# Layer 0's up-projection by Strassen's seven products, activations through DRAM, down-projection as a stage of its own

## The chip, the cores and the metric

One core of a Trainium2 chip runs the whole program as one launch. The metric is device time in microseconds (us): the median of the runs, beside a profile of one execution. Engines: PE is TensorE's matmul, PEld its weight load, DVE is VectorE, ACT is ScalarE, POOL is GpSimd, SP issues most of the DMAs.

## The reference, cut to what matters

Two layers work on 512 latent tokens and 256 context tokens with a model width of 1024. Each layer has a token mixing part (gated linear attention, window attention, pooling, one output projection) and a channel mixing part. Only the second is touched:

```python
def conv_ffn(h, w_up, conv_w, conv_b, w_down):      # h: tokens x 1024, w_up: 1024 x 5632, w_down: 2816 x 1024
    u = h @ w_up
    up = jnp.pad(u, ((0, 0), (1, 1), (0, 0)))
    u = up[:, :-2] * conv_w[0] + up[:, 1:-1] * conv_w[1] + up[:, 2:] * conv_w[2] + conv_b
    a, g = jnp.split(u, 2, axis=-1)
    return (jax.nn.silu(g) * a) @ w_down
...
h2 = rms_norm(x, norm2_g) * (1 + sc2) + sh2
x = x + g2 * conv_ffn(h2, w_up, conv_w, conv_b, w_down)
```

In layer 0 this runs over latents and context; in layer 1 over latents alone, since the context is no longer wanted. All data are float32.

## The kernel before, in words

Activations lie feature-major: a tile has 128 features on the partitions and the tokens along the free dimension, 512 latent columns and then 258 for the context (256 with a zero on either side, which the convolution needs). A float32 product is done in three passes of TensorE's rounded float32 type: each operand is split into a rounded part (hi) and the rest (lo), and hi*hi, hi*lo and lo*hi are added up in PSUM (acc3, L540). A weight tile is 128 x 1024: SP loads it into wst, ACT copies it to whi with rounding, DVE subtracts to wlo (wjob, L497). The normed activations are split when they are made (make_h, L763).

The channel mixing of layer 0 goes by 22 pairs j of a value tile and a gate tile (128 columns of w_up each). A pair takes two steps, one for each half of the 1024 rows (up, L1845; pairjob, L531). A step has 2 tiles x 4 k-tiles x 3 passes, and each of those is one matmul on the 512 latent columns and one on the 258 context columns: 96 matmuls a pair. Then conv (L1813) takes the tile out of PSUM (one ACT instruction for the middle tap and the bias, two on DVE for the outer taps), up_done (L1830) applies SiLU on ACT, multiplies on POOL, and splits the product into ahi (ACT) and alo (DVE), which stay in SBUF. After each group of pairs (FF_GROUPS: 2, 4, 4, 4, 4, 4) down_chunk (L1850) multiplies the group by its rows of w_down and adds the result to the residual x in SBUF; the pairs run two ahead of the groups (N_UP). Products go to three pairs of PSUM banks in turn (nbb3, L253). Between these steps stand single chunks of the modulation product of layer 1 (tick, L634: one 512 KB load and 32 x 128 columns on TensorE), which accumulate in a seventh bank. Before the first pair, norm2 (L1791) works out 1/rms and make_h the eight pairs of tiles of h; after the last group next_stats (L1911) sums the squares for the next norm.

Two things set the order. From the start to norm2, and from next_stats on, the tensor engine keeps the order of emission, which the kernel plans with estimated times; within the channel mixing (ordered(False) to ordered(True), L1928) the framework's scheduler orders every engine at compile time by its own estimate. Steps load their weights two jobs ahead (run_steps, L471, AHEAD). All SBUF tiles of 770 columns are slabs of one pool of 44 (slab, L218); a slab is free when its last reader is done. Weight rings and tables are constant tiles.

Of the kernel before, what the change touches and what calls it, by code (L numbers as in the profile page):

```python
# [8 lines left out]
F32 = mybir.dt.float32  # L9
# [5 lines left out]
ALU = mybir.AluOpType  # L15
# [16 lines left out]
SW = 770  # L32
# [33 lines left out]
N_WHI = 3  # L66
AHEAD = 2
# [5 lines left out]
FF_GROUPS = (2, 4, 4, 4, 4, 4)  # L73
LAT = slice(0, 512)
# [14 lines left out]
class Estimate:  # L89
    """Estimated times (us) of the engines and of the columns of the tiles. They only serve to choose  # L90
    an order of emission on the tensor engine in which it seldom waits."""
# [30 lines left out]
    def last(self, ap, kinds, eng=None):  # L122
        """time at which the last access (kinds: w, r) to the columns of ap is over, as seen by eng"""
# [21 lines left out]
class Engine:  # L145
    """An engine whose instructions also advance its estimated clock."""
# [27 lines left out]
    def _account(self, fname, args, kw):  # L174
# [22 lines left out]
        # what waits for a load lets the others pass  # L197
# [8 lines left out]
def trunk_kernel(ctx: ExitStack, tc: tile.TileContext, a, out, dbg=None):  # L206
# [6 lines left out]
    slabs = ctx.enter_context(tc.tile_pool(name="slabs", bufs=NSLAB))  # L213
    tiny = ctx.enter_context(tc.tile_pool(name="tiny", bufs=3))
# [6 lines left out]
    class Ring:  # L221
        """Fixed buffers taken in turn; reuse is ordered by the accesses themselves."""
# [9 lines left out]
    wad = Ring(const, N_WAD, 1024, F32, "wad")  # L232
    whi = Ring(const, N_WHI, 1024, F32R, "whi")
    wlo = Ring(const, N_WHI, 1024, F32R, "wlo")
    wst = Ring(const, N_WST, 1024, F32, "wst")
# [8 lines left out]
    class Pair:  # L244
        """latent and context halves of a product; whole where they lie in one tile"""
# [15 lines left out]
    # ---------------------------------------------------------------- constants  # L261
# [8 lines left out]
    scanm = const.tile([128, 512], F32, name="scanm")  # L270
    rope_c = const.tile([128, 4, 64], F32, name="rope_c")
    rope_s = const.tile([128, 4, 64], F32, name="rope_s")
    inve = const.tile([128, 2, 33], F32, name="inve")
    zbuf = const.tile([128, 512], F32, name="zbuf")
    G.memset(zbuf, 0.0)
# [3 lines left out]
    def load_tables():  # L279
        def load(**kw):  # L280
            after(SP.dma_start(**kw), start["il"])
        load(out=rope_c, in_=a["k_cos"].rearrange("(t p) d -> p t d", p=128))
        load(out=rope_s, in_=a["k_sin"].rearrange("(t p) d -> p t d", p=128))
# [6 lines left out]
        load(out=scanm, in_=a["k_scan"])  # L290
# [11 lines left out]
    gqk = const.tile([128, 512], F32, name="gqk")  # L302
    sink = const.tile([128, 6], F32, name="sink")
    nsink = const.tile([128, 6], F32, name="nsink")
    xdram = dram.tile([KD, 128, XW], F32, name="xdram")

    # ---------------------------------------------------------------- helpers
    def rstd_act(ss, inv_n, n=None):
        """(ss * inv_n + eps)^-0.5 from ScalarE's logarithm and exponential, refined by one step"""
# [46 lines left out]
    def warm(t):  # L356
        """keeps the tensor engine's clock up until t: idle, it falls to half its rate"""
# [545 lines left out]
    def layer(l):  # L903
# [946 lines left out]
        def down_chunk(j0, nk, mp, final):  # L1850
            def fn(hi, lo):
                if final:
                    bnext.load(3)
# [178 lines left out]
```

## Time and profile before

| | |
|---|---|
| median of 3 runs | 1647.62 us (1647.1 to 1647.99) |
| span of the profiled execution | 1645.8 us |
| TensorE busy / granted clock | 1607.5 us (98%) / 0.995 |
| VectorE, ScalarE, GpSimd busy | 947.4, 639.1, 268.4 us |
| channel mixing of layer 0 on TensorE | 401.7 to 971.9 us |

The profiled execution's own time is its span, from its first to its last instruction; the times of the runs hold a little more, 1647.62 - 1645.8 = 1.8 us at the median. A busy TensorE in this profile is not one at its peak, since the ends of matmuls are modelled: the pace is read from the distance of their starts. Start, duration and count stand in the rows of a timeline; a row "x2" merges two instructions.

### The profile page before, as it was taken

The page shows a single profiled execution, that of the slowest core. Times are in us where ns is not written, and L with a number is a line of the kernel's source. Part 1 is how long each engine was busy: PE and PEld are TensorE (multiplying, and loading weights), DVE is VectorE, ACT ScalarE, POOL GpSimd, SP SyncE. Part 2 cuts the span into 40 slices and gives each one's busy share as a digit, 9 for nine tenths or more (in the row PEclk, how much of TensorE's full clock was granted, in tenths as well). Part 3 has the DMA queues.
Part 4 walks back from the last instruction along what each step waited for, and adds up shares of the span by engine and source line. Part 5 has one row for each costly group of instructions (what it writes and reads, how often), then busy time and mean ns, then how long its engine had stood idle before and what let it go on. Part 6 is the DMA issues. An engine that isn't in the chain of part 4 may idle for free. (4 is left out here: it accounts for less than half of the span.)

```text
span 1645.8 us, 24715 instructions
## 1 busy us (share of the span) xinstructions
PE 1607.5 (98%) x9659; PEld 1308.3 (79%) x9659; DVE 947.4 (58%) x1730; ACT 639.1 (39%) x1174; POOL 268.4 (16%) x342
## 2 busy tenths in 40 slices
PE   7999999999999999999999999999899999999998
PEld 4777778787878888888888876778777888888886
DVE  6576477876554434434344364877785655545555
ACT  4354254554322313223132342654564433433331
POOL 1105034434100101001010041121302000000000
PEclk9999999999999999999999999999999999999999
DMA  9943352214243122221222275223232233233322
GB/s 324 236 146 112 114 161 59 81 40 154 77 130 89 64 65 65 65 65 52 64 64 65 89 252 156 62 67 112 66 104 78 70 110 103 91 95 97 102 90 77
DMA packets 206977, 169.12 MB, mean 103 GB/s; under 512 B 30616, under 2 KB 183715, under 8 KB 206860
## 3 DMA queue, kind: packets, MB, share of 16 engines
q1 hardware_dynamic: 204364, 158.74, 32.4%
q0 software_dynamic: 2496, 8.79, 1.5%
q8 instruction: 76, 1.25, 0.3%
q14 instruction: 41, 0.34, 0.1%
HBM read 160.15 MB, written 7.35 MB: 102 GB/s over the span
## 5 line engine op out<-in xcount | busy, mean ns | idle before, releaser
L155 ACT CAST whi<-wst 128x1024 fp32r<-128x1024 f32 (+3 forms) x202 | 201.2, 997 | 416.6 <-PE dbl L367 253.3
L155 DVE TENSOR_TENSOR wlo<-wst,whi 128x1024 fp32r<-128x1024 f32 (+1 forms) x177 | 218.0, 1232 | 181.9 <-ACT whi L155 179.8
L367 PE MATMUL dbl<-hlo,whi 128*128 128x512 f32 (+1 forms) x720 | 219.7, 357 | 0.0
L367 PE MATMUL dbl<-hhi,wlo 128*128 128x512 f32 x720 | 219.2, 357 | 0.0
L367 PE MATMUL dbl<-hhi,whi 128*128 128x512 f32 x720 | 218.2, 358 | 0.0
L155 POOL TENSOR_TENSOR cv<-cv 128x770 f32<-128x770 f32 (+1 forms) x44 | 69.4, 1578 | 816.1 <-ACT cv L155 806.2
L367 PE MATMUL sgl<-hhi,whi 128*128 128x512 f32 (+1 forms) x568 | 192.0, 367 | 1.0 <-ACT hhi L155 1.0
L367 PE MATMUL sgl<-hlo,whi 128*128 128x512 f32 (+1 forms) x568 | 186.3, 355 | 0.0
L367 PE MATMUL sgl<-hhi,wlo 128*128 128x512 f32 (+1 forms) x568 | 185.3, 355 | 0.0
L155 DVE SCALAR_TENSOR_TENSOR cv<-dbl,cwT,cv 128x769 f32<-128x769 f32 (+1 forms) x120 | 105.9, 883 | 58.7 <-ACT cv L155 56.7
L367 PEld LDWEIGHTS dbl<-hhi,whi 128*128 128x128 f32 x720 | 120.3, 189 | 22.8 <-issue 1.6
L367 PEld LDWEIGHTS dbl<-hlo,whi 128*128 128x128 f32 x720 | 120.1, 188 | 21.3
L367 PEld LDWEIGHTS dbl<-hhi,wlo 128*128 128x128 f32 x720 | 119.6, 188 | 21.0 <-issue 0.4
L367 PEld LDWEIGHTS sgl<-hhi,whi 128*128 128x128 f32 x568 | 100.1, 188 | 27.5 <-issue 10.4
L155 DVE SCALAR_TENSOR_TENSOR x<-dbl,modT,x 128x256 f32<-128x256 f32 (+1 forms) x105 | 65.2, 648 | 89.7 <-PE dbl L367 89.2
L367 PEld LDWEIGHTS sgl<-hlo,whi 128*128 128x128 f32 x568 | 100.5, 189 | 15.9 <-issue 0.5
L367 PEld LDWEIGHTS sgl<-hhi,wlo 128*128 128x128 f32 x568 | 100.2, 189 | 15.8
L367 PE MATMUL dbl<-alo,whi 128*128 128x512 f32 x342 | 103.8, 358 | 0.0
L367 PE MATMUL dbl<-ahi,whi 128*128 128x512 f32 x342 | 103.7, 358 | 0.0
L367 PE MATMUL dbl<-ahi,wlo 128*128 128x512 f32 x342 | 103.7, 358 | 0.0
L155 DVE TENSOR_TENSOR alo<-cv,ahi 128x770 fp32r<-128x770 f32 (+1 forms) x44 | 36.3, 825 | 110.2 <-ACT ahi L155 110.2
L155 DVE SCALAR_TENSOR_TENSOR x<-sgl,modT,x 128x256 f32<-128x256 f32 (+1 forms) x88 | 55.0, 641 | 54.0 <-PE sgl L367 53.5
(276 smaller groups left out, 2890.2 us busy)
## 6 DMA issues: line engine op xcount, KB each, us to landing
wst<-in_w_up SPq DMA_DIRECT2D x176, 256.0 KB, 3.3
adaw<-in_w_ada SPq DMA_DIRECT2D x96, 256.0 KB, 5.3
wad<-in_w_ada SPq DMA_DIRECT2D x48, 512.0 KB, 3.8
wst<-in_w_down SPq DMA_DIRECT2D x40, 512.0 KB, 3.4
wst<-in_w_in SPq DMA_DIRECT2D x26, 512.0 KB, 4.0
wst<-in_w_out SPq DMA_DIRECT2D x32, 192.0 KB, 3.3
xdram<-x SPq DMA_DIRECT2D x8, 385.0 KB, 6.0
x<-xdram POOLq DMA_DIRECT2D x8, 385.0 KB, 4.6
```

Of the source, the lines that this page charges most:

```text
L155: r = real(*args, **kw)
L367: T.matmul(o, w, m, start=start, stop=stop, **kw)
```

## The change

- The product for pairs 3 to 21 is a 2 x 2 block product: the rows of w_up in two halves, the value and the gate tile as the two columns, and the tokens in two halves of 386 columns (latents 0 to 385; latents 386 to 511, a zero, the context, a zero). Strassen's scheme (Winograd's form) takes seven products of blocks for the eight of the plain one, each of 4 k-tiles x 3 passes on 386 columns, and pays with sums: four of weights (S1 to S4) on GpSimd, four of activations (T1 to T4, made once), and per pair seven of results on the way out of PSUM. Pairs 0 to 2 run as plain products on the same 386 columns, while T1 to T4 are made.
- S1 to S4 are split into hi and lo like the weights X11, X12 and X22: 3584 columns a pair are cast and subtracted, where it was 2048.
- The activation of a pair is no longer split at once: it goes to DRAM (adram, by GpSimd's queue). The residual x goes to DRAM as well (xdram) while the norm is applied. After the last pair, all is loaded again by SP's queue; the activations are split then, and the down-projection runs in three groups (8, 8, 6).
- Weight rings and four tables share a pool of 13 tiles of 128 x 1024. In the Strassen stage its tiles hold the weights and their sums; the tables are loaded again afterwards. Weights are loaded one job ahead in that stage. The modulation chunks run in the plain steps and in the down-projection.
- Layer 1 keeps its code.

```diff
+        def make_y(R):
...
+            for k in range(KD):
+                SP.dma_start(out=xdram[k], in_=xs[k][:, 0:XW])
+            for p in range(4):
+                r, q = p // 2, p % 2
+                t1, t2 = f[r, q] = new7(f"Y{r + 1}1"), new7(f"Y{r + 1}2")
+                for i in range(2):
+                    k, o = 2 * p + i, HH * i
+                    for g, t, c, x in ((0, t1, o, slice(0, HH)), (0, t2, o, slice(HH, 512)), (1, t2, o + 513 - HH, CTX)):
+                        d = t[:, c:c + x.stop - x.start]
+                        V.scalar_tensor_tensor(d, in0=xs[k][:, x], scalar=amod[l][:, g, 1, k:k + 1], in1=R[:, x],
+                                               op0=ALU.mult, op1=ALU.mult)
+                        A.activation(d, d, func=AF.Identity, bias=modT[l][:, g, 24 + k:25 + k])
...
+        def products7(bank, w, n):
+            for k in range(4):
+                (wh, wl), (yh, yl) = w[k], yk(n, k)
+                for i, (w_, m_) in enumerate(((wh, yh), (wh, yl), (wl, yh))):
+                    mm(bank, w_, m_, start=k == 0 and i == 0, stop=k == 3 and i == 2)
...
+        def job7(j):
+            def load():
...
+                for half in range(2):
+                    t = wide(name="raw")
+                    for m, c0 in enumerate((128 * j, FF + 128 * j)):
+                        SP.dma_start(out=t.rearrange("p (k m n) -> p k m n", k=4, m=2)[:, :, m, :],
+                                     in_=rows(w_up, 512 * half, 4, c0, 128))
...
+                def split(src, h, l_):
+                    A.copy(h, src)
+                    V.tensor_tensor(l_, src, h.bitcast(F32), op=ALU.subtract)
...
+                split(xa[:, :, 0, :], cut(ua[:, 0:512]), cut(la[:, 0:512]))
+                G.tensor_tensor(q1, xa[:, :, 1, :], xb[:, :, 1, :], op=ALU.add)
+                G.tensor_tensor(q2, q1, xa[:, :, 0, :], op=ALU.subtract)
+                G.tensor_tensor(q4, xb[:, :, 0, :], q2, op=ALU.subtract)
+                G.tensor_tensor(q3, xa[:, :, 0, :], xa[:, :, 1, :], op=ALU.subtract)
...
+                split(s14[:, :], h14[:, :], l14[:, :])
+                split(raw[0][:, :], hb[:, :], lb2[:, :])
+                split(s23[:, 0:256], ua[:, 512:768], la[:, 512:768])
+                split(s23[:, 256:1024], ub[:, 0:768], lb[:, 0:768])
...
+        sets7 = [(dbl[0], dbl[1]), (sgl2, dbl[0])] + [((dbl[1], sgl2), (msc2, dbl[0]))[j % 2] for j in range(2, KF)]
...
+        def gated(j, ta, tg):
+            x = slice(1, 1 + XW)
+            s["silu_f"] = A.activation(tg[:, x], tg[:, x], func=AF.Silu)
+            G.tensor_tensor(ta[:, x], ta[:, x], tg[:, x], op=ALU.mult)
+            G.dma_start(out=adram[j], in_=ta[:, x])
...
+        def up7(j):
...
+                products7(a0, w["X11"], "Y11")
+                A.copy(t1, a0)
+                products7(g0, w["S1"], "T1")
+                A.copy(t5, g0)
+                products7(a1, w["S2"], "T2")
+                V.tensor_tensor(u2, a1, t1, op=ALU.add)
+                G.tensor_tensor(t5, t5, u2, op=ALU.add)
+                products7(g1, w["S3"], "T3")
+                V.tensor_tensor(t7, g1, u2, op=ALU.add)
+                A.copy(u2, t5)
+                products7(a0, w["X12"], "Y21")
+                products7(g0, w["X22"], "T4")
+                for p, x in halves(bg, (vb, 0)):
+                    V.tensor_tensor(p, p, x, op=ALU.add)
+                tg = conv7(KF + j, bg)
+                products7(a1, w["S4"], "Y22")
+                for p, x in halves(bv, (va, 0)):
+                    V.tensor_tensor(p, p, x, op=ALU.add)
+                gated(j, conv7(j, bv), tg)
...
+        def acts(j0, nk):
+            for j in range(j0, j0 + nk):
+                t, hi, lo = slab(name="af"), slab(F32R, name="ahi"), slab(F32R, name="alo")
+                SP.dma_start(out=t[:, 0:XW], in_=adram[j])
+                A.copy(hi[:, 0:XW], t[:, 0:XW])
+                V.tensor_tensor(lo[:, 0:XW], t[:, 0:XW], hi[:, 0:XW].bitcast(F32), op=ALU.subtract)
...
+            def back():
...
+                new_tables()
+                acts(0, DN_GROUPS[0])
+                for k in range(KD):
+                    x = slab(name=f"x{k}")
+                    SP.dma_start(out=x[:, 0:XW], in_=xdram[k])
+                    s["xs"].append(x)
+                fill_tables(SP.dma_start)
```

conv7 is conv on the two halves: where the two banks are one tile, each of its three instructions covers both (772 columns), else there are two of 386 columns.

## Rows read from the trace of the kernel before

**Rows 1.** The page: span, and busy time of each engine.

```profile
span 1645.8 us, 24715 instructions
PE 1607.5 (98%) x9659; PEld 1308.3 (79%) x9659; DVE 947.4 (58%) x1730; ACT 639.1 (39%) x1174; POOL 268.4 (16%) x342
```

**Rows 2.** Busy time by stage: stretch, its length, busy us of five engines, clock, DMA.

```profile
401.70:971.90 570.20, 570.20 (x3273) 491.36 (x3270) 262.28 (x341) 166.93 (x200) 59.33 (x63) 1.00 0.28 85
```

**Rows 3.** Groups of TensorE by shape in that stretch: count, busy us, mean ns.

```profile
L367 PE MATMUL dbl<-hhi,whi 128*128 128x512 f32 x240 | 95.7, 399 | 0.0
...
L367 PE MATMUL sgl<-hhi,whi 128*128 128x512 f32 x112 | 44.7, 399 | 0.0
```

**Rows 4.** Timeline of TensorE, first and last of 16 rows: start, us, count.

```profile
600.42 0.51 PE L367 MATMUL sgl<-hhi,whi 128*128 128x512 f32 x2
...
605.72 0.51 PE L367 MATMUL dbl<-hhi,whi 128*128 128x512 f32 x2
```

**Rows 5.** Timeline of TensorE in layer 0's attention: two matmuls on 384 columns.

```profile
294.22 0.52 PE L367 MATMUL dbl<-KT,QT 128*128 128x384 f32 x2
294.58 0.28 PE L367 MATMUL dbl<-bandb,identb 128*128 128x128 bf16 x2
```

**Rows 6.** Groups of VectorE by shape, 470 to 920 us; the last row whole span.

```profile
L155 DVE TENSOR_TENSOR wlo<-wst,whi 128x1024 fp32r<-128x1024 f32 x52 | 63.5, 1222 | 64.0 <-ACT whi L155 64.0
L155 DVE SCALAR_TENSOR_TENSOR cv<-dbl,cwT,cv 128x769 f32<-128x769 f32 x48 | 48.9, 1018 | 42.4 <-ACT cv L155 41.5
L155 DVE SCALAR_TENSOR_TENSOR cv<-sgl,cwT,cv 128x511 f32<-128x511 f32 x22 | 16.4, 744 | 21.9 <-ACT cv L155 21.9
L155 DVE TENSOR_TENSOR alo<-cv,ahi 128x770 fp32r<-128x770 f32 x17 | 16.3, 960 | 50.9 <-ACT ahi L155 50.9
L155 DVE SCALAR_TENSOR_TENSOR cv<-sgl,cwT,cv 128x257 f32<-128x257 f32 x22 | 10.5, 477 | 0.0
...
L155 DVE TENSOR_TENSOR raw<-dbl,gqk 128x512 f32<-128x512 f32 x8 | 5.5, 686 | 2.8 <-ACT qsq L155 2.7
```

**Rows 7.** Groups of ScalarE by shape, 470 to 920 us.

```profile
L155 ACT CAST whi<-wst 128x1024 fp32r<-128x1024 f32 x52 | 54.6, 1049 | 190.4 <-PE dbl L367 125.6 <-PE sgl L367 64.8
L155 ACT ACTIVATE cv<-dbl,vecT,cwT 128x770 f32<-128x770 f32 x24 | 23.9, 994 | 44.4 <-PE dbl L367 44.4
...
L155 ACT CAST ahi<-cv 128x770 fp32r<-128x770 f32 x17 | 14.2, 838 | 32.6 <-POOL cv L155 32.6
```

**Rows 8.** Groups of GpSimd by shape, whole span.

```profile
L155 POOL TENSOR_TENSOR cv<-cv 128x770 f32<-128x770 f32 x22 | 40.7, 1851 | 486.1 <-ACT cv L155 486.1
L155 POOL TENSOR_TENSOR cv<-cv 128x512 f32<-128x512 f32 x22 | 28.7, 1305 | 330.0 <-ACT cv L155 320.1 <-issue 9.9
```

**Rows 9.** Timelines of VectorE and GpSimd where their work meets.

```profile
385.71 1.55 DVE L155 TENSOR_TENSOR wlo<-wst,whi 128x1024 fp32r<-128x1024 f32 x1 [0.88 <-ACT whi L155]
...
957.00 3.97 DVE L155 TENSOR_TENSOR wlo<-wst,whi 128x1024 fp32r<-128x1024 f32 x1 [1.24 <-ACT whi L155]
...
957.16 0.75 POOL L155 TENSOR_TENSOR acc<-acc,sq 128x256 f32<-128x256 f32 x1
...
957.90 1.98 POOL L155 TENSOR_TENSOR acc<-acc,sq 128x512 f32<-128x512 f32 x2
```

**Rows 10.** Timeline of VectorE in make_h: its first and last rows.

```profile
398.36 1.14 DVE L155 SCALAR_TENSOR_TENSOR ht<-x,amod,R 128x512 f32<-128x512 f32 x2
...
416.49 1.54 DVE L155 SCALAR_TENSOR_TENSOR hlo<-ht,modT,hhi 128x256 fp32r<-128x256 f32 x3
```

**Rows 11.** The page: DMA issues (count, KB each, us to landing), and bandwidth by slice.

```profile
GB/s 324 236 146 112 114 161 59 81 40 154 77 130 89 64 65 65 65 65 52 64 64 65 89 252 156 62 67 112 66 104 78 70 110 103 91 95 97 102 90 77
...
wst<-in_w_up SPq DMA_DIRECT2D x176, 256.0 KB, 3.3
...
x<-xdram POOLq DMA_DIRECT2D x8, 385.0 KB, 4.6
```

**Rows 12.** The page: a group of weight loads (count, busy us, mean ns).

```profile
L367 PEld LDWEIGHTS dbl<-hhi,whi 128*128 128x128 f32 x720 | 120.3, 189 | 22.8 <-issue 1.6
```

More of the change, by code (lines that the diff above doesn't have):

```diff
@@ L73 @@
 FF_GROUPS = (2, 4, 4, 4, 4, 4)
+DN_GROUPS = (8, 8, 6)
+HH = 386
+HW = 2 * HH
 LAT = slice(0, 512)
@@ L1791, in norm2, with yk @@
+        def yk(n, k):
+            hi, lo = s["y"][n][k // 2]
+            c = slice(HH * (k % 2), HH * (k % 2) + HH)
+            return hi[:, c], lo[:, c]
         def norm2():
@@ L1798, in norm2 @@
             ring3[0] = 2
-            s["h"] = ([], [])
-            make_h(l, 1, s["xs"], range(KD), s["h"], R, with_ctx=full)
+            if full:
+                make_y(R)
+            else:
+                s["h"] = ([], [])
+                make_h(l, 1, s["xs"], range(KD), s["h"], R, with_ctx=False)
             bub2.run(BB2[2])
@@ L1853, in fn @@
                     bnext.load(3)
-                pss = [nbb3() for _ in range(2)]
+                if first:
+                    s["pd"] = [nbb3() for _ in range(2)]
+                pss = s["pd"]
                 for m in range(2):
@@ L1873, in down_chunk, with bubble_next, alloc_acc, ffn7 @@
             return fn
+        def bubble_next():
+            bub[0] = bnext = Bubble(N_BA if full else 0)
+            def alloc_acc():
+                s["h"] = s["y"] = None
+                s["acc2"] = []
+                if full:
+                    after(A.preload_act_table_set("natural_log_exp_and_others"), s["silu_f"])
+            step(alloc_acc)
+            return bnext
+        def ffn7():
+            nonlocal bnext
+            for j in range(N_STD):
+                for half in range(2):
+                    if 2 * j + half == 2 * N_STD - 1:
+                        step(lambda: ahead_by.__setitem__(0, 1))
+                    step(up_std(j, half), pairjob(w_up, half, 128 * j, FF + 128 * j, j + half == 0))
+                    if not getattr(ada_q[0][1], "first", False):
+                        tick(1)
+                    tick(0)
+                    if j == 0 and half or j == 1 and not half:
+                        step(lambda q=j: make_t(q))
+            assert ada_q[0][1].first
+            for j in range(N_STD, KF):
+                step(up7(j), job7(j))
+            def back():
+                s["h"] = s["y"] = None
+                s["xs"] = []
+                ahead_by[0] = AHEAD
+                new_tables()
+                acts(0, DN_GROUPS[0])
[4 more added lines that the diff above has]
+                fill_tables(SP.dma_start)
+            step(back)
+            j0 = 0
+            for gi, nk in enumerate(DN_GROUPS):
+                final = gi == len(DN_GROUPS) - 1
+                if final:
+                    bnext = bubble_next()
+                parts = [(j0, 4), (j0 + 4, nk - 4)]
+                for mp in range(4):
+                    for i, (q0, n) in enumerate(parts):
+                        step(down_chunk(q0, n, mp, final, i == 0, i == len(parts) - 1),
+                             wjob((kview(n, 256), rows(w_down, 128 * q0, n, 256 * mp, 256)), n=256 * n))
+                        tick(1 if len(ada_q) > 37 else 0)
+                    if mp == 1 and not final:
+                        step(lambda q=j0 + nk, n=DN_GROUPS[gi + 1]: acts(q, n))
+                j0 += nk
         def out_rows(m):
```

215 lines of the change are left out of this document (170 added, 45 removed).

## The prediction

> **What bounds the kernel now.** I read the page first: TensorE is busy 98% of the span, VectorE 58% [rows 1]. Shares over the whole span hide stages, so the second view is the busy time by stage. In the channel mixing of layer 0, from 401.7 to 971.9 us, TensorE is busy for all of its 570.2 us at the full clock, while VectorE has 262, ScalarE 167 and GpSimd 59 us [rows 2]. The third view, the groups by shape, gives what it does there: 352 steps (240 + 112) of the first pass on 512 columns, that is 22 pairs x 2 tiles x 8 k-tiles [rows 3]. The fourth is the pace, from starts and not from durations. From 600.42 to 605.72 us there are 15 intervals of one latent and one context matmul each, so 5.30 / 15 = 0.3533 us for 512 + 258 columns [rows 4]. The stage is bound by the number of columns that stream through TensorE, and nothing waits there. A change that takes matmuls out shortens it one for one, as long as the others keep the new pace.
>
> **The matmuls (the gain).** Before, a pair has 48 intervals: 48 x 0.3533 = 16.96 us. After, a Strassen pair has 7 x 4 x 3 = 84 matmuls of 386 columns. 386 is the mean of 512 and 258 but for one column, so I take half an interval, 0.1767 us: 84 x 0.1767 = 14.84 us. The nearest row on one size is 384 columns, two in 294.58 - 294.22 = 0.36 us, 0.18 each [rows 5]; it gives 15.12 us. Gain a pair 2.12 us (1.84 by that row), times 19 pairs: 40 us (35). The plain pairs have 96 x 0.1767 = 16.96 us, as before (17.28, +1 us for three by the other row). The down-projection keeps its matmuls and the modulation its chunks. Term: **-40 us**, between -34 and -40.
>
> **Work of the other engines in a Strassen pair.** TensorE must not be kept waiting in 14.84 us.
>
> VectorE [rows 6]. Five subtractions of SBUF by SBUF (512, 1024, 1024, 256, 768 columns): 1.22 for 1024 and 0.96 for 770 make 1.03 ns a column and 0.16 us fixed, so 3584 columns and 5 instructions are 4.5 us. Two sums of 386 columns out of PSUM at about 0.55 (from 0.69 for 512), 1.1 us; adding them to the banks, one of 772 and two of 386, about 2.1 us; the convolution's outer taps, two of 772 at 1.02 and four of 386 at 0.61 (between 0.48 for 257 and 0.74 for 511), 4.5 us. In all 12.2 us, or 82%; before it was 46% in this stage.
>
> ScalarE [rows 7]: casts of 3584 columns 4.0, three copies of 386 columns 1.6, the middle taps 0.99 + 2 x 0.67, SiLU 0.85: 8.8 us, 59%.
>
> GpSimd [rows 8]: four sums of 512 columns at 1.31, one of 386 at 1.04, the product of 770 at 1.85: 8.1 us, 55%, and a DMA issue; before, 59 us in 570, 10% [rows 2].
>
> Each fits. The trouble is that VectorE and GpSimd do not run freely beside each other. A subtraction of 1024 columns that takes 1.22 us alone took 1.55 us at 385.71 and 3.97 us at 957.00; the latter ended only after GpSimd's three sums of 957.16 to 959.88 us [rows 9]. SBUF subtractions and GpSimd's sums (4.5 and 8.1 us a pair) then follow one another, 12.6 us of 14.84; the 7.7 us that read PSUM may lie beside GpSimd. If a subtraction finds GpSimd at work 7 times in 10 and waits for half of a sum of 1.3 us, that is 5 x 0.7 x 0.65 = 2.3 us, and VectorE stands at 14.5 of 14.84 us. An engine so full and in order is sometimes late, and what is queued behind its wait are the sums that free a bank for the seventh product, and the lo parts of the next weights. There is slack: three products (6.4 us) lie between the reading of a bank and its next use, and the next pair has the other four banks. I take 0.5 us a pair, 9.5 us. Bounds: 0, as the load fits; and 3.8 us a pair, if each of five subtractions waits out a whole sum (12.2 + 6.5 = 18.7 us), 72 us. I stay near the lower end, because two of the three rows nearest to it show a wait of nothing to a third of a microsecond: 1.22 as the mean of 52 and 1.55.
>
> The Trainium skill says of this, in "SBUF — State Buffer", section "Who interferes with whom", that a VectorE instruction with two SBUF inputs and a GpSimd instruction that reads SBUF exclude one another, and that the second to issue fully blocks. The 3.97 us agree with it. By that rule alone the change is charged with a collision for every subtraction that comes second; what that would make of the time is the rival on the other side, below.
>
> **The start of the stage.** In make_h VectorE worked from 398.36 to 418.03 us at 2.25 us a k-tile (one weight split of 1.2 us among them), and TensorE needed 2.12 for each [rows 4, 10]. make_y has three pieces a k-tile (386, 126, 256 columns: 0.61 + 0.34 + 0.48) and a subtraction of 772 at 0.96, 2.4 us; ScalarE casts besides, about 2.3 us. The tiles are finished some 3 us later, in twos from the third on, and pair 1 can fill only with its value tile, since pair 0 holds four banks. **+3 us**, between 0 and 8 (eight tiles of 2.4 us and all of the last chunk in the open). The sums T1 to T4 (6 on GpSimd, 10 subtractions or sums on VectorE of 0.96) lie beside 51 us of plain pairs and cost nothing; without that cover they would cost about 10 us.
>
> **The first Strassen weights.** They need tiles that the plain steps still hold. From load to the second product's lo part: 3.3 us of DMA [rows 11], three sums of 1.31, a cast of 1.05, a subtraction of 1.22, 9.5 us, against 8.5 us for the last plain step. **+2 us**, 0 to 9.5.
>
> **From the last pair to the down-projection.** The activations 0 to 7 were written long before; their loads (4.6 us for 385 KB [rows 11]), casts (0.84) and subtractions (0.96) can start when the products of the last pair free the slabs of Y and T. If nothing is early, the first costs 6.4 us, and 16 loads of 385 KB, 6.2 MB, take 19 us at the best slice's 324 GB/s [rows 11] with weights queued behind them on SP, which TensorE has 8.5 us of work to hide. **+5 us**, 0 to 17. The write of the residual, the tables and 17 MB more of DMA lie beside a stage that uses 28% of its DMA time [rows 2], at no cost; the fewer residual additions of the down-projection (3 instead of 6 for each tile) return nothing, as TensorE ends last there.
>
> **Sum.** -40 + 9.5 + 3 + 2 + 5 = -20.5 us against the profiled span of 1645.8 [rows 1]: 1625.3, and with the 1.8 us by which the median of the runs lies above it, **1627 us**.
>
> **The rivals.**
>
> *TensorE stays the bound (forecast), 0.60.* All terms between their low ends and about half of the high ones: 1647.6 - 40 = 1608 to 1640.
>
> *VectorE, blocked by GpSimd, becomes the bound (the other side), 0.22.* Place: the subtractions of the weights in pairs 3 to 21. For it: the waits [rows 9], a load of 82% without them, and GpSimd's four sums that start with the same load as the first subtraction. Against it: most subtractions show none of it, and PSUM reads may lie beside GpSimd. Price: if one subtraction a pair waits out a run of sums, as at 957 us (2.75 us), and four wait half a sum each (2.6), VectorE needs 12.2 + 5.4 = 17.6 us a pair, 2.7 above TensorE: 51 us. With the edges, 1647.6 - 40 + 51 + 10 = 1669 us. It decides from a period of 14.84 + (40 - 10) / 19 = 16.4 us on: there the change is slower. The section of the Trainium skill named above is the rule behind it.
>
> *The edges of the stage cost their upper bounds, 0.11.* 8 + 9.5 + 17 instead of 10: 1627 + 24.5 = 1651.5 with all three; with the two largest 1646.5; with the load alone 1639. For it: no row shows the pool in this use. Against it: the slabs become free product by product during 14.8 us. I put it at 1642 us.
>
> *386 columns do not run at the mean, 0.07.* Each matmul has its own weight load, and one shows 0.19 us [rows 12]; if that were the pace on 386 columns, 84 x 0.19 = 16.0 us, a gain of 1.0 a pair, 19 us, less 4 us in the plain pairs and 10 at the edges: 1643 to 1648 us, no change. Against it: 258 columns already start the next matmul far sooner, or no interval of 0.3533 us for two could be [rows 4], and 384 columns take 0.18 [rows 5].
>
> **How the numbers follow.** Predicted is the likeliest case, 1627 us; its own range is 1608 to 1640. The range that is to hold the time 8 times in 10 takes in the edges and the lower part of the rival on the other side: 1608 to 1660. A measurement of this kernel cannot tell 0.2%, 3.3 us, from no change. Faster: 0.60, with most of the edges' and part of the pace's share, 0.70. Same: 0.08. Slower: 0.22.
>
> **What would show it.** In the changed profile the starts of 386-column matmuls lie 0.177 us apart; a Strassen pair takes 14.8 to 15.4 us; TensorE's idle time in the stage is under 25 us, and the largest gaps are at its start, before the first Strassen pair and before the first down-projection. Subtractions of weights on VectorE have a mean above their 1.22 us for 1024 columns. The prediction is wrong if VectorE is busy for over 95% of the Strassen stage and TensorE waits for lo parts or banks in each pair, if the period is over 16.4 us, or if one edge costs over 17 us.

## The result and the profile after

The changed kernel takes 1625.97 us (median of 4 runs, 1621.44 to 1627.44) where the kernel before took 1647.8 beside it: ratio 0.9858, 95% interval 0.9841 to 0.9874. The forecast was 1627. Its profiled execution took 1625.49 us, with a span of 1623.7, against 1625.3 in the sum of the prediction.

The page of the changed kernel: its span and each engine's busy time.

```profile
span 1623.7 us, 24874 instructions
PE 1571.5 (97%) x9431; PEld 1317.8 (81%) x9431; DVE 1054.4 (65%) x1860; ACT 706.2 (43%) x1321; POOL 426.1 (26%) x510
```

TensorE lost 228 matmuls, 12 for each of 19 pairs [rows 1], and stays the busiest engine. Layer 0's channel mixing, from the first `acc,ones` matmul of its norm to that of layer 1's, went from 581.4 us to 556.6 (390.49 to 947.04): 24.9 less. Layer 1, whose code did not change, went from 674.0 to 676.7: 2.7 more. Together that is, but for rounding, the 22.1 us between the two spans [rows 1].

Busy time of five engines in stretches of the Strassen stage, then clock, DMA share and GB/s; this answers to [rows 2].

```profile
470.00:740.00 270.00, 265.94 (x1497) 264.12 (x1496) 223.53 (x280) 137.32 (x210) 163.70 (x159) 1.00 0.34 98
500.00:550.00 50.00, 50.00 (x284) 50.00 (x284) 41.20 (x53) 25.77 (x39) 26.50 (x25) 1.00 0.36 103
600.00:650.00 50.00, 50.00 (x285) 50.00 (x284) 44.31 (x54) 24.33 (x37) 31.52 (x27) 1.00 0.28 88
```

In the two stretches without a wait 284 and 285 matmuls start in 50 us: 0.1757 us each, so 14.8 us a pair. In 270 us TensorE stands still for 4.1. VectorE went from 46% to 83%, GpSimd from 10% to 61%.

To see where the time went I added up, for the stage of both kernels, the intervals from each matmul's start to the next and compared each with the median of its kind. The up-projection falls by 29.6 us (374.2 to 344.6); 228 matmuls fewer at 0.177 would be 40.4. Of its 344.6 us, 11.1 lie above 0.177 us a matmul: 4.7 at the first Strassen pair, 5.3 in the pairs behind it, and 1.1 in the plain pairs, most of it beside modulation chunks, where the kernel before loses about as much. The wait in the norm ahead of the stage adds 3.5, the down-projection 1.2 (188.6 after 187.4), and the rest is 0.0 in sum. Together -24.9.

### The profile page after: what moved, and what is told of

It reads as the page before. It is cut to its first block, busy times and chain, and to the rows that moved or that the text cites. A ratio compares the mean times of both kernels' runs of the same rounds, so it can differ in the third digit from the quotient of the medians.

```text
span 1623.7 us, 24874 instructions
## 1 busy us (share of the span) xinstructions
PE 1571.5 (97%) x9431; PEld 1317.8 (81%) x9431; DVE 1054.4 (65%) x1860; ACT 706.2 (43%) x1321; POOL 426.1 (26%) x510
## 3 DMA queue, kind: packets, MB, share of 16 engines
q8 instruction: 74, 1.21, 0.3%
## 5 line engine op out<-in xcount | busy, mean ns | idle before, releaser
L401 PE MATMUL sgl<-hhi,whi 128*128 128x512 f32 (+1 forms) x344 | 132.0, 384 | 2.6 <-ACT cv L160 1.6
L401 PE MATMUL sgl<-hhi,wlo 128*128 128x512 f32 (+1 forms) x344 | 125.8, 366 | 0.0
L401 PE MATMUL sgl<-hlo,whi 128*128 128x512 f32 (+1 forms) x344 | 125.6, 365 | 0.0
L160 DVE SCALAR_TENSOR_TENSOR cv<-dbl,cwT,cv 128x511 f32<-128x511 f32 (+1 forms) x106 | 91.3, 862 | 7.9 <-ACT cv L160 6.8
L401 PE MATMUL dbl<-hhi,wlo 128*128 128x512 f32 x240 | 94.6, 394 | 0.0
L401 PE MATMUL dbl<-hlo,whi 128*128 128x512 f32 x240 | 94.0, 392 | 0.0
L401 PE MATMUL dbl<-hhi,whi 128*128 128x512 f32 x240 | 93.2, 394 | 0.0
L160 POOL TENSOR_TENSOR wlo<-wst,whi 128x640 fp32r<-128x640 f32 (+2 forms) x25 | 42.8, 1712 | 157.4 <-ACT whi L160 157.4
L401 PEld LDWEIGHTS sgl<-hhi,wlo 128*128 128x128 f32 x344 | 64.8, 188 | 11.3
L160 POOL TENSOR_TENSOR s<-raw 128x512 f32<-128x512 f32 x38 | 55.1, 1469 | 44.2 <-DMA raw<-in_w_up 38.4
L401 PEld LDWEIGHTS dbl<-ahi,whi 128*128 128x128 f32 x346 | 57.1, 188 | 10.9 <-issue 0.8
L401 PEld LDWEIGHTS dbl<-alo,whi 128*128 128x128 f32 x346 | 57.2, 189 | 10.1
```

What stands on the lines that cost most here:

```text
L160: r = real(*args, **kw)
L401: T.matmul(o, w, m, start=start, stop=stop, **kw)
```

## The experiments

All ratios are to the kernel before, run beside each.

**The same kernel again.** No edit; its spread from execution to execution is to be known.

> The changed kernel once more, on the chip of the three runs beside it, as their base. Expected by every theory: 1626 us within 4, ratio to before 0.986; in its trace the same three waits: about 3 us on the last sums of squares, about 2.5 us ahead of the first Strassen pair with a stretch at the lower clock behind it, and under 7 us in all inside the Strassen pairs.

1625.19 us (1623.58 to 1629.23), ratio 0.9847 (0.9831 to 0.9863), span 1623.0, with the same waits at the same places: 2.3 us in the norm (3.3 in the first execution), 2.5 us ahead of the first Strassen pair with a half-clock stretch behind it, 3.4 us inside the pairs (4.1). Differences of 2 us between two medians are therefore not told apart by time alone; below, a term of that size is read from its place in the trace.

**No Strassen pair.** All 22 pairs are plain, in the new stage, layout and DRAM path.

```diff
-N_STD = 3
+N_STD = KF
...
             def back():
+                tab.clear()
...
                 new_tables()
```

> All 22 pairs as plain products on 2 x 386 columns; everything else of the change stays (activations through DRAM, three groups in the down-projection, T1 to T4 are still made though nobody reads them). Theory A, the gain is the 12 matmuls that each Strassen pair leaves out and the rest of the change costs a little: 1626 + 19 x 2.12 us - 5.7 us of waits in the Strassen pairs - 4.5 us ahead of the first = 1656 us, slower than before by 0.5%. Rival B, the separate down-projection or the even halves bring part of it: at 1648 us or below.

1656.61 us, ratio 1.0034 (1.0021 to 1.0047). The new frame without Strassen is slower than the kernel before; the seven products are what pays, with 31 us for 19 pairs, 1.6 each of the 2.1 gross. It also settles the rival on 386 columns: the 22 plain pairs of this run take 373.9 us on 386 columns and took 374.2 on 512 and 258.

**Twelve plain pairs.** 10 Strassen pairs instead of 19.

```diff
-N_STD = 3
+N_STD = 12
```

> Twelve plain pairs and ten by Strassen in place of 3 and 19. Theory A: 9 pairs x (2.12 - 0.3 us of waits) more than the changed kernel, 1626 + 16 = 1642 us, and the same wait or less ahead of the first Strassen pair, since T1 to T4 have long been made. Rival B, the gain is not by the pair: under 1634 us. Rival C, VectorE is late in each pair and its backlog grows along the stage: more than half of the gain is lost, over 1646 us.

1642.93 us, ratio 0.9958 (0.9941 to 0.9976): where the first theory had it, but ten executions spread from 1638.07 to 1651.81, and the profiled one is the fastest of them. Busy times in three stretches of it: plain pairs, Strassen pairs, start of the down-projection.

```profile
470.00:600.00 130.00, 130.00 (x738) 130.00 (x737) 56.47 (x69) 43.59 (x54) 25.04 (x28) 1.00 0.28 88
630.00:740.00 110.00, 109.70 (x620) 109.39 (x619) 95.94 (x115) 56.24 (x86) 68.35 (x66) 1.00 0.32 97
760.00:770.00 10.00, 8.14 (x44) 6.78 (x43) 6.18 (x10) 4.57 (x6) 0.00 (x0) 1.00 0.80 273
```

VectorE is busy 43% in plain and 87% in Strassen pairs, and TensorE waits 0.3 us in seven of the latter. Nothing waits ahead of the first one either (613.8 us). But the down-projection now starts with waits, 1.9 us in ten, for activations loaded from DRAM, with the DMA share at 0.80: nine plain pairs more remove the wait at the first Strassen pair, and a wait at the last edge appears that the changed kernel does not have.

**The writes of the residual, later.** The 8 DMAs `xdram<-x` stood in SP's queue ahead of the norm's end; they are moved behind the last scaling of make_y.

```diff
-            for k in range(KD):
-                SP.dma_start(out=xdram[k], in_=xs[k][:, 0:XW])
...
-                        V.scalar_tensor_tensor(d, in0=xs[k][:, x], ...
+                        last_y = V.scalar_tensor_tensor(d, in0=xs[k][:, x], ...
...
+            for k in range(KD):
+                after(SP.dma_start(out=xdram[k], in_=xs[k][:, 0:XW]), last_y)
```

> The eight writes of the residual to DRAM are put behind the last instruction of the norm that reads the residual, instead of ahead of it; nothing else changes. Theory A, the 3 us on the last sums of squares are a weight load that shares the DMA engines with these writes and holds up ScalarE's queue: that wait goes, 1626 - 3 = 1623 us, and nothing is late in its place. Rival D, the load is late because of the modulation weights that are loaded in the same stretch: no change, 1626 us. Rival E, the writes now collide with the loads for the next plain pairs: the 3 us come back behind 404 us of the trace.

> The version with the residual's writes behind make_y, again and with more rounds. It should lie 2 to 4 us below the changed kernel's 1625 to 1626: 1622 to 1623.5, ratio 0.982 to 0.9855 against the kernel before. If the gain seen once was run-to-run variation, it comes back to 1625 to 1627.

1622.86 us, ratio 0.9823 (0.9807 to 0.9839), and in the second set 1622.65, 0.9836 (0.982 to 0.9852). Both lie some 2.5 us below the changed kernel; the intervals overlap, so the proof is the place in the trace, and not the time. Timelines of the changed kernel at the start of the stage (start, us, engine, what, and in brackets the idle time before and what ended it), and DMA share there:

```profile
371.11 1.40 SPq L160 DMA_DIRECT2D xdram<-x  x2
...
387.20 1.00 SPq L160 DMA_DIRECT2D wst<-in_w_up  x2
...
395.43 1.04 ACT L160 CAST whi<-wst 128x1024 fp32r<-128x1024 f32 x1 [4.35 <-DMA wst<-in_w_up]
396.38 0.41 ACT L160 ACTIVATE acc<-x 128x256 f32<-128x256 f32 x1
...
396.85 0.70 PE L401 MATMUL dbl<-acc,ones 128*128 128x256 f32 x2 [3.27 <-ACT acc L160]
...
403.76 0.62 PE L401 MATMUL dbl<-hY,whi 128*128 128x386 f32 x2 [1.44 <-ACT hY L160]
...
390.00:404.00 14.00, 8.11 (x81) 3.97 (x80) 7.46 (x16) 5.47 (x11) 1.67 (x20) 1.00 1.10 313
```

The same with the later writes (second set):

```profile
392.17 1.03 ACT L160 CAST whi<-wst 128x1024 fp32r<-128x1024 f32 x1
393.10 0.41 ACT L160 ACTIVATE acc<-x 128x256 f32<-128x256 f32 x1
...
401.61 0.62 PE L401 MATMUL dbl<-hY,whi 128*128 128x386 f32 x2 [1.44 <-ACT hY L160]
...
390.00:404.00 14.00, 11.17 (x122) 6.35 (x123) 9.20 (x22) 7.68 (x18) 3.53 (x21) 1.00 0.28 84
```

A weight load issued at 387.20 lands at 395.4, in a stretch whose DMA share is 1.10; ScalarE stands in order at its cast, and behind the cast stands the last square of the norm, for which TensorE waits 3.27 us. With the writes moved, the cast waits for nothing, that wait is gone, and none comes in its place behind 404 us. From the first `acc,ones` (390.49 and 391.68) to the first product it is 13.27 us in the one and 9.93 in the other. The writes did two things that this run doesn't part: they shared the DMA engines with the load, and they held it back in SP's queue, for with the later writes the same load is issued at 381.91 and not at 387.20.

**More GpSimd work in a pair.** Four sums of 512 columns on activations are added after S1 to S4, into a tile that nobody reads.

```diff
+                y_ = s["y"]["Y11"][0][0][:, 0:512].bitcast(F32)
+                for _ in range(4):
+                    G.tensor_tensor(tkr.t[0], y_, y_, op=ALU.add)
```

> Four more sums of 512 columns on GpSimd for each Strassen pair, of an activation tile into a buffer that nobody reads; the rest is the changed kernel. Theory A, subtractions of SBUF tiles on VectorE and sums on GpSimd exclude one another: 4.5 + 8.1 + 4 x 1.31 = 17.8 us have to follow one another in a pair, against 14.84 of TensorE: 19 x 3 = 56 us more, 1682 us, and waits of TensorE in every pair. Rival F, each engine bears its own load: GpSimd stands at 13.3 us and a DMA issue, under 14.84: no change, 1626 us within 5.

1672.15 us (two executions), ratio 1.0132 (1.0112 to 1.0153): 46 us more, 2.4 a pair for 5.0 us of GpSimd work (1.25 a sum). Busy times, then two of VectorE's groups by shape (count, busy us, mean ns):

```profile
470.00:740.00 270.00, 247.00 (x1324) 242.93 (x1325) 228.43 (x252) 123.17 (x189) 209.43 (x194) 0.95 0.26 81
...
L160 DVE TENSOR_TENSOR la<-raw,ua 128x512 fp32r<-128x512 f32 x17 | 35.7, 2102 | 0.0
...
L160 DVE TENSOR_TENSOR l<-s,h 128x1024 fp32r<-128x1024 f32 x15 | 26.2, 1746 | 1.0 <-ACT h L160 1.0
```

VectorE's own instructions are the same, yet the subtraction of 512 columns takes 2.10 us and that of 1024 1.75 (1.22 and 1.21 in the changed kernel). Work on GpSimd lengthens work on VectorE: this is the rival on the other side, made to happen by one added load. Of TensorE's 30.0 us of waits from 455 to 760 us, 18.0 are for VectorE, which is busy 85% of the time. Not all of the 46 us is that: the half-clock stretches behind the waits (mean clock 0.95) come on top, and what GpSimd's own lateness adds, with 5 us more a pair in its queue, was not parted from it.

**The opposite: no sums on GpSimd.** S1 to S4 are not computed; plain blocks of the weights stand in, so the output is not the reference's.

```diff
-                G.tensor_tensor(q1, xa[:, :, 1, :], xb[:, :, 1, :], op=ALU.add)
-                G.tensor_tensor(q2, q1, xa[:, :, 0, :], op=ALU.subtract)
-                G.tensor_tensor(q4, xb[:, :, 0, :], q2, op=ALU.subtract)
-                G.tensor_tensor(q3, xa[:, :, 0, :], xa[:, :, 1, :], op=ALU.subtract)
...
-                split(s14[:, :], h14[:, :], l14[:, :])
+                split(raw[0][:, :], h14[:, :], l14[:, :])
```

> The four sums of weights on GpSimd are left out (S1 to S4 are replaced by plain blocks of w_up, cast and subtracted as many columns as before), so the output is not the reference's; matmuls and all other work stay. Theory A, the meeting of the two engines costs TensorE nearly nothing in the Strassen pairs (5.7 us of waits in all), since VectorE's delay hides behind the products: 1626 - 5 = 1621 us, subtractions back at their time alone (0.68 us for 512 columns). Rival G, the delay of VectorE costs more than the waits show, as work that is late elsewhere: 1612 us or less.

1647.65 us, ratio 0.9989 (0.998 to 0.9998): a miss for both, 22 us slower than with the sums. Busy times and two groups, of ScalarE and of VectorE (the last column is the idle time before, and what ended it):

```profile
470.00:740.00 270.00, 257.67 (x1437) 252.92 (x1436) 215.77 (x270) 132.66 (x203) 71.56 (x87) 1.00 0.31 93
...
L160 ACT CAST h<-raw 128x1024 fp32r<-128x1024 f32 x17 | 17.8, 1047 | 42.8 <-DMA raw<-in_w_up 42.8
...
L160 DVE TENSOR_TENSOR lob<-raw,hb 128x1024 fp32r<-128x1024 f32 x18 | 33.0, 1832 | 0.0
```

The row of `lob` (1.83 us, alone 1.22) shows that collisions remain, with GpSimd's gated product and its sum of two copies. In fact they cost as much as before: the five subtractions of a pair take 6.18 us by their means, 6.19 in the changed kernel and 4.5 alone. But ScalarE stands 42.8 us before the cast `h<-raw`, waiting for its load: the edit also made the casts read the raw tiles last, so the next load starts later. The experiment changed two things, so its time says nothing on what the sums cost.

**The sums replaced by loads.** To part the two, the tiles of the sums are filled by DMA with plain blocks (again not the reference's output), and the raw tiles come free as before.

```diff
-                G.tensor_tensor(q1, ...   (and q2, q4, q3)
+                for half, t in enumerate((s14, s23)):
+                    for m, c0 in enumerate((128 * j, FF + 128 * j)):
+                        SP.dma_start(out=t.rearrange("p (k m n) -> p k m n", k=4, m=2)[:, :, m, :],
+                                     in_=rows(w_up, 512 * half, 4, c0, 128))
```

> The four GpSimd sums of weights are left out and the two tiles that held them are filled by DMA with plain blocks of w_up instead (the output is not the reference's); the raw tiles come free as early as in the changed kernel, unlike in the run without sums, and every cast, subtraction and matmul stays. DMA per Strassen pair doubles from 1 to 2 MB. Theory A (GpSimd's sums and the shared port make the waits inside the pairs): the subtractions fall to 1.22 us for 1024 columns, the waits inside the pairs from 5.7 to under 2 us, the wait ahead of the first Strassen pair shrinks too; 1626 - 4 to -7 = 1619 to 1622. Theory B (the waits come from the order in the queues and from tiles that come free late, whatever GpSimd does): the subtractions get shorter, but TensorE still waits 5 us or more in the pairs, 1624 to 1630. Theory C (late weight loads made the run without sums slow): with double the loads the waits on ScalarE for raw tiles come back, 1640 or more.

1632.43 us, ratio 0.9895 (0.9876 to 0.9914), above the ranges of the first two theories and below the third's. Busy times, two groups, and the waits of TensorE by what ended them (us, times, longest):

```profile
470.00:740.00 270.00, 261.31 (x1453) 257.40 (x1452) 216.52 (x275) 136.15 (x205) 65.32 (x87) 0.99 0.57 160
...
L160 ACT CAST h<-s 128x1024 fp32r<-128x1024 f32 x17 | 17.9, 1050 | 32.6 <-DMA s<-in_w_up 32.6
...
PE dbl L401 <- ACT pa L160: 4.3, 2, 2.2
PE dbl L401 <- DVE pb L160: 2.1, 4, 0.8
PE sgl L401 <- ACT pa L160: 2.0, 2, 1.4
```

GpSimd works 65 us instead of 164, but the five subtractions of a pair still take 5.97 us by their means, and TensorE waits longer (8.7 us for 4.1), mostly for ScalarE's copies of products (`pa`), which free a bank. They stand in ScalarE's queue behind a cast that waits for a late tile. So a GpSimd with 65 us of work costs VectorE nearly as much as one with 164: all 25.5 us that 84 subtractions lose fall on the 29 that start while a sum or product of GpSimd is running. Late loads spoil this run's time too. What the waits would be with GpSimd idle and the weights on time was not measured.

**VectorE in place of GpSimd for one sum.** On top of the later writes, the sum of two product copies goes to VectorE.

```diff
-                G.tensor_tensor(t5, t5, u2, op=ALU.add)
+                V.tensor_tensor(t5, t5, u2, op=ALU.add)
```

> The version with the late writes, and the sum of two product copies (386 columns, once per Strassen pair) goes from GpSimd to VectorE. Theory J: the waits inside the pairs come from queues in order and not from load: GpSimd's gated product holds up this sum, ScalarE waits for it, and the copy that frees the next bank stands behind it on ScalarE (654.96: 2.2 us). Without GpSimd in that chain the waits on ScalarE's copies go (TensorE idles under 2 us inside the pairs instead of 5.8): 1622.6 - 4 = 1618 to 1620, although VectorE gets 0.5 us more per pair. Theory A (VectorE's fullness and the shared port make the waits): VectorE stands at 15 of 14.8 us, the waits grow, 1625 to 1632. Theory K (any edit reshuffles the queues, and the sum of the waits comes out somewhere between 4 and 12 us): 1622 to 1629, with waits at other places.

1630.13 us, ratio 0.9888 (0.9871 to 0.9904), 7.5 above the version that it changes. Busy times, the moved sum, and TensorE's longest row of waits:

```profile
470.00:740.00 270.00, 262.19 (x1471) 259.67 (x1470) 248.87 (x296) 138.58 (x208) 143.45 (x141) 1.00 0.33 95
...
L160 DVE TENSOR_TENSOR pa<-pa,pb 128x386 f32<-128x386 f32 x18 | 23.3, 1292 | 0.3
...
PE dbl L401 <- DVE pb L160: 5.6, 6, 1.6
```

The sum, expected at 0.5 us, takes 1.29 on VectorE beside GpSimd's work; sums of the same 386 columns with one operand in PSUM take 0.56. VectorE stands at 92%, and TensorE now waits for it in every second pair (602.96, 633.60, 664.22, 694.98, 726.54 us: eight pairs in 123.6 us, 15.4 each). The waits for ScalarE's copies are gone, as the theory of order had it, but waits for VectorE, which it did not have, more than take their place. The share of VectorE alone does not say when that happens: with twelve plain pairs it was at 87% with next to no wait, with four plain pairs (below) at 83% all 6.5 us of TensorE's waits from 470 to 740 us were for it.

**Three ways at the first Strassen pair**, all on top of the later writes: a fourth plain pair; the gated product of the plain pairs on VectorE; the sum T3 on VectorE.

```diff
-N_STD = 3
+N_STD = 4
```

> The late writes of the residual, and four plain pairs in place of three. Theory A, the wait ahead of the first Strassen pair (2.5 us and 1.7 us of a stretch at the lower clock) is T1 to T4 not being done in time in ScalarE's and GpSimd's queues: one more plain pair covers it and costs 2.1 us: 1623 - 4.2 + 2.1 = 1621 us. Rival H, the wait is for tiles of the weight pool that the plain steps hold: it stays, 1625 us.

```diff
-            G.tensor_tensor(ta[:, x], ta[:, x], tg[:, x], op=ALU.mult)
+            (V if j < N_STD else G).tensor_tensor(ta[:, x], ta[:, x], tg[:, x], op=ALU.mult)
```

> The late writes of the residual, and the product of SiLU and value in the three plain pairs on VectorE instead of GpSimd. Theory A, GpSimd's queue stood still for 7.3 us before that product while T3 and T4 were queued behind it: the wait ahead of the first Strassen pair goes or shrinks to under 1 us, 1623 - 3.5 = 1619 us. Rival I, VectorE, which is 84% busy there, becomes late instead: no change or slower, 1623 us or more.

```diff
-            G.tensor_tensor(t3[:, x], y22[:, x], y12[:, x], op=ALU.subtract)
+            V.tensor_tensor(t3[:, x], y22[:, x], y12[:, x], op=ALU.subtract)
```

> As the version with the late writes, but the sum of T3 (two per 256 rows, 772 columns) goes from GpSimd to VectorE, which has room in the plain pairs. If GpSimd's queue of T sums behind pair 0's product is what makes the first Strassen pair wait: the wait shrinks from about 2.5 us plus the stretch at half clock to under 1, 1623 - 3 = 1620. If the order that the scheduler gives the queues sets the waits, other waits appear in its place: 1622 to 1628.

1626.35 (0.9851; 0.9835 to 0.9867), 1629.52 (0.9876; 0.9861 to 0.989) and 1623.43 (0.9837; 0.9823 to 0.9852): none beats the later writes alone. From 404 to 950 us TensorE waits 8.1 us with the later writes alone. The first takes the wait ahead of that pair away, but comes to 9.7 in all; the second keeps it (2.2 us) and comes to 11.3. In the third the cause is seen to be right and the gain is given back. The queues of the changed kernel at the first Strassen pair:

```profile
445.02 2.88 POOL L160 TENSOR_TENSOR cv<-cv 128x770 f32<-128x770 f32 x1 [7.30 <-ACT cv L160]
...
448.83 1.86 POOL L160 TENSOR_TENSOR fT<-fY,fY 128x772 f32<-128x772 f32 x1
450.63 1.29 POOL L160 TENSOR_TENSOR s<-raw 128x512 f32<-128x512 f32 x1
451.89 1.81 POOL L160 TENSOR_TENSOR fT<-fY,fT 128x772 f32<-128x772 f32 x1
...
453.73 0.84 ACT L160 CAST hT<-fT 128x772 fp32r<-128x772 f32 x1 [2.17 <-POOL cv L160]
454.47 0.61 ACT L160 CAST ua<-raw 128x512 fp32r<-128x512 f32 x1
...
455.14 0.45 PE L401 MATMUL msc<-hY,ua 128*128 128x386 f32 x1 [2.52 <-ACT ua L160]
```

GpSimd waits 7.30 us for the product of a plain pair, with the sums T behind it in order; ScalarE waits for a T tile (the row's wait is put down to `cv`, but the cast reads `fT`, which GpSimd ended at 453.70), and behind that stands the cast that the first Strassen pair needs. With T3 on VectorE the first Strassen matmul starts at 450.09 without a wait, and the wait that follows is 0.95 us. But then this appears in a later pair:

```profile
620.64 0.48 ACT L160 COPY pa<-msc 128x386 f32<-128x386 f32 x1
...
621.17 0.44 PE L401 MATMUL msc<-hY,hb 128*128 128x386 f32 x1 [4.11 <-ACT pa L160]
```

The copy stands behind three casts (618.67 to 620.7), as one did behind two in the changed kernel at 654.96. Which of them comes first in ScalarE's queue is fixed by the order of the program, and here the edit elsewhere shifted it. But the casts are only the last link. Timelines of GpSimd, ScalarE and TensorE in the changed kernel:

```profile
645.66 1.85 POOL L160 TENSOR_TENSOR cv<-cv 128x770 f32<-128x770 f32 x1 [6.75 <-ACT cv L160]
647.47 2.98 POOL L160 TENSOR_TENSOR s<-raw 128x512 f32<-128x512 f32 x2
650.40 0.13 POOL L160 MEMSET cv<- 128x2 f32 x2
...
650.53 0.67 ACT L160 ACTIVATE cv<-sgl,vecT,cwT 128x386 f32<-128x386 f32 x1 [4.45 <-POOL cv L160]
...
654.43 0.47 ACT L160 COPY pa<-msc 128x386 f32<-128x386 f32 x1
...
654.96 0.44 PE L401 MATMUL msc<-hY,hb 128*128 128x386 f32 x1 [2.17 <-ACT pa L160]
```

ScalarE itself stood still for 4.45 us, until GpSimd had set the edge columns of a `cv` tile to zero. That is 0.13 us of work, but it stands in GpSimd's queue behind the product and two sums, and GpSimd had been idle for 6.75 us ahead of the product. With T3 on VectorE ScalarE waits 4.46 us for the same step (615.34). So both waits begin in GpSimd's queue. No run moves this small step to another engine or place; what that would give is not shown. Above 0.177 us a matmul the pairs behind the first lose 5.3 us in the changed kernel, 7.6 and 5.5 in two executions of the version with later writes, and 10.5 and 10.0 with T3 or the sum of two copies on VectorE.

## Why the prediction came out

**Matmuls: -40, right.** 0.1757 us for 386 columns where 0.1767 was taken; without what is lost at the first Strassen pair and in those behind it, the up-projection falls by 39.6. TensorE stays the bound, and the run without Strassen shows that nothing else in the change pays.

**Work in the pairs: +9.5 predicted, 5.3 measured.** The five longest intervals between starts in the pairs are 0.6, 0.5, 1.2, 2.5 and 0.9 us where 0.18 is usual; what they hold above that is 4.8 of the 5.3. VectorE's groups by shape in the changed kernel, 470 to 740 us, the five subtractions (count, busy us, mean ns):

```profile
L160 DVE TENSOR_TENSOR lb<-s,ub 128x768 fp32r<-128x768 f32 x17 | 24.5, 1442 | 0.0
L160 DVE TENSOR_TENSOR lob<-raw,hb 128x1024 fp32r<-128x1024 f32 x17 | 23.0, 1353 | 0.3 <-ACT hb L160 0.3
L160 DVE TENSOR_TENSOR la<-raw,ua 128x512 fp32r<-128x512 f32 x17 | 20.8, 1222 | 0.4 <-ACT ua L160 0.4
...
L160 DVE TENSOR_TENSOR l<-s,h 128x1024 fp32r<-128x1024 f32 x17 | 20.6, 1211 | 0.0
...
L160 DVE TENSOR_TENSOR la<-s,ua 128x256 fp32r<-128x256 f32 x17 | 16.3, 959 | 10.0 <-ACT ua L160 9.9
```

Without GpSimd beside them they would take about 0.95, 1.22, 0.69, 1.22 and 0.42 us (by [rows 6]); collisions cost 0.5, 0.1, 0.5, 0 and 0.5 us, together 1.7 a pair, predicted 2.3. Singly: 34 of these 85 subtractions meet no sum or product of GpSimd and take their time alone within 0.01 us; the 36 that start while one is running bear 23.4 of the 29.1 us lost. The collisions exist, and they hide: VectorE is busy 83% of the time, not the 98% of the estimate. All rows of that view add up to 238 us in 18 pairs, 13.2 each, against a forecast of 14.5; and the engine is occupied for 223.5, as one instruction can start up to 0.1 us before the one ahead of it has ended. The margin was wider than estimated, and it is not endless: the sum moved to VectorE used it up. The step also named the wrong chain. Of 4.1 us that TensorE waits in the pairs, 3.3 are for ScalarE's copies, the two longest (2.2 and 0.9) after ScalarE had itself waited for steps in GpSimd's queue, and 0.8 for VectorE.

**Start of the stage: +3 predicted; 3.5 measured.** The size is right, the mechanism is not. (The 2.25 us a k-tile that it took for make_h is the distance in the middle of it; all of 398.36 to 418.03 us is 2.46 a k-tile, 2.3 without the weight split.) What is late is not make_y, whose tiles cost 1.44 us ahead of the first product, with or without the moved writes; it is a weight load beside the residual's writes, which the prediction costed at nothing by the share of DMA over the whole stage (28%, [rows 2]). In the 14 us that count the share is 1.10, and the writes also stand ahead of the load in SP's queue. In the kernel before, the slices of [rows 11] already show 154 GB/s there (the tenth, 370 to 411 us) and 65 in the middle of the stage; read by slice, the term could have been there.

**T1 to T4 at nothing, first weights +2: together 4.7.** The wait of 2.52 us with a small one behind it, and 1.7 lost at half clock after it. The load was on time; the sums T, which were taken to be hidden by 51 us of plain pairs, were late. They had time enough, but not their own: in GpSimd's queue they stand behind a product that comes only at the end of a plain pair.

**Last pair to down-projection: +5 predicted, no wait.**

```profile
749.06 0.34 PE L401 MATMUL msc<-hY,l 128*128 128x386 f32 x1
749.24 0.51 PE L401 MATMUL sgl<-ahi,whi 128*128 128x512 f32 x2
...
749.81 0.34 PE L401 MATMUL dbl<-hT,ub 128*128 128x386 f32 x1
```

In this timeline of TensorE the first steps of the down-projection stand between the products of the last pair: the first tiles were loaded from 734.53 us on, so the down-projection has something to do while the others load. All of the down-projection together costs 1.2 us more than before. That this is a matter of order shows in two other runs, which wait 1.8 and 2.6 us there.

**Layer 1: not in the sum, +2.7.** A wait of 1.6 us at 1263.92 that is not in the kernel before, and one half-clock stretch more. No code differs there, but TensorE and ScalarE have a few instructions in another order; that this makes the wait is not shown.

The sum of the prediction was -20.5, the two spans differ by -22.1. The 1.6 between them is made, but for rounding, of +0.4 in the matmuls, -4.2 in the pairs, -3.8 at the last edge (1.2 for 5), +0.5 at the start, +2.7 at the first pair and +2.7 in layer 1. The mechanism and its largest term are shown; that the total is so near is luck, as errors of 14 us in size stand against each other. Of its signs one came out in part (of the two subtractions of 1024 columns one has a mean above 1.22 us, 1.35, and one does not, 1.21), and one did not: no gap stands ahead of the down-projection.

**The rivals.** VectorE as the bound: not here, but in two experiments most of TensorE's waits are for it, one with 5.0 us of GpSimd work more a pair (1.013), one with a single sum of 386 columns more on VectorE. The Trainium skill, in "SBUF — State Buffer", section "Who interferes with whom", gives the rule: of a VectorE instruction with two SBUF inputs and a GpSimd instruction that reads SBUF the second to issue is blocked. The traces agree: without the sums on GpSimd, all 28.4 us that 85 subtractions lost fell on the 27 that started while GpSimd was at work, and none on the 12 during which it began. The 386-column sum with both inputs in SBUF takes 1.29 us, those with one in PSUM 0.56, and with four sums more on GpSimd only instructions of VectorE with two SBUF inputs grew, four of the five subtractions. By that rule alone one could not tell the outcome, which hung on the room left. Edges at their upper bounds: refuted, 9.4 in sum (3.5 + 4.7 + 1.2) and not 34.5. Pace of 386 columns: refuted by the run without Strassen.

**Best version.** The changed kernel with the residual's writes behind make_y: 0.9823 and 0.9836 in two sets. By time alone it cannot be told from the changed kernel (0.9858 and 0.9847); by the trace the wait of 3.3 us is gone.

## What to carry to other kernels

Work that is removed from the engine that bounds pays one for one only where nothing waits: here 40.4 us of matmuls gave 22.1. Count the occupied time of every other engine with its collisions, but do not read the outcome from its share: at 83 to 87% VectorE cost next to nothing in some versions and made TensorE wait in others. Follow a wait back through every engine's queue to the first that was late; here that was often a small step on GpSimd. A step "hidden beside 51 us of other work" is hidden only if nothing ahead of it in its own queue waits; look up what stands in front of it, and read the DMA share in the slice where a load is due and not over the stage. When changing what one queue holds, expect waits of 1 to 4 us at other places, and repeat the timing before calling such an edit a gain.

## What was unexpected in the hardware

After a wait of some 2.5 us the granted clock of TensorE can fall for a while: in the changed kernel, behind the wait that ends at 455.14, stretches from 455.1 show

```profile
455.10:458.00 2.90, 2.76 (x11) 2.42 (x12) 2.77 (x6) 2.90 (x5) 1.70 (x2) 0.78 0.03 6
458.00:460.20 2.20, 2.20 (x9) 2.20 (x8) 2.20 (x4) 1.76 (x4) 2.20 (x4) 0.52 0.00 0
460.20:465.00 4.80, 4.80 (x29) 4.80 (x28) 4.80 (x7) 3.16 (x4) 1.23 (x2) 1.00 0.00 2
```

a clock near 0.5, the lower of its two levels (1.2 GHz), at which matmuls of 386 columns start 0.32 us apart (nine intervals from 456.98 to 459.87) instead of 0.18; the stretch cost 1.7 us. Of the version with the later writes, one execution had it (a wait of 2.27 us ending at 454.63, then a clock of 0.51 until 458.0) and the other not (2.52 us at 453.01, then 1.00); nor did it follow the 3.27 us at 396.85 in the changed kernel. A wait's price therefore varies from one execution to the next; how much of the spread of about 6 us between runs of the changed kernel comes from that is not shown. That two queues in order, SP's and ScalarE's, pass a late load on to a norm that has nothing to do with it was the other surprise: 8 writes of 385 KB cost 3.3 us of TensorE through one cast. And between GpSimd and VectorE the order of the starts decides: in the two runs without sums of weights on GpSimd, the 56 subtractions that started while it was at work lost 53.9 us, and the 18 beside which it began later lost nothing.
